# Gated delta rule in a hybrid mixer block: products of two heads that alternate between row tiles, a recurrence on full 128x128 tiles, and the masked q.k products written as one run

## The chip, the cores and the metric

The kernel runs on one core of a Trainium2 chip. A core has a matrix engine (TensorE, PE in the profile; its weight loads are listed apart as PEld), VectorE (DVE), ScalarE (ACT), GpSimd (POOL) and SyncE (SP), each with a queue of its own that it works off in order. The metric is the device time of one execution in microseconds.

## The reference, cut to what matters

One layer for 512 tokens of width 1024: a norm, a wide projection, four token mixers side by side (a gated delta rule, latent attention, gated linear attention, forgetting attention), gates and a merge, an output projection, and a two-layer MLP. The change touches the gated delta rule, with 4 heads of 64 channels and 8 chunks of 64 tokens:

```python
def gated_delta_rule(q, k, v, g, beta):           # chunks of C = 64 tokens
    gc = cumsum(g over the chunk)
    diff = gc[..., :, None] - gc[..., None, :]
    decay_ts = where(lower, exp(diff), 0)
    kk = einsum('bhncd,bhnsd->bhncs', kc, kc)
    a_strict = where(strict, beta * kk * decay_ts, 0.0)
    # (u | w) = (I + a_strict)^-1 (v * beta | k * beta * exp(gc))
    qk = einsum('bhncd,bhnsd->bhncs', qc, kc) * decay_ts
    q_decay = qc * exp(gc);  k_tail = kc * exp(gc[-1] - gc);  chunk_decay = exp(gc[-1])

    def step(state, inp):                          # one chunk after the other
        v_new = u_c - einsum('bhck,bhkv->bhcv', w_c, state)
        o_c = einsum('bhck,bhkv->bhcv', qd_c, state) + einsum('bhcs,bhsv->bhcv', qk_c, v_new)
        state = state * cd_c + einsum('bhck,bhcv->bhkv', kt_c, v_new)
        return state, o_c
```

## The kernel before

Everything is float32. Large projections are split into high and low parts and computed as three products of 512 columns (mm3, L246, weights whi and wlo; the cast that makes whi is L149 on ScalarE, the subtraction that makes wlo is L150 on VectorE). Small products are plain float32; each of them is two passes on TensorE, which the profile counts as two matmuls. A product may use the whole 128x128 array, or a part of it: a row tile of 64 rows (64\*128 in the rows) when the contraction has 64 elements, or a column tile (128\*64) when the output has 64 partitions. Which part is chosen follows from the partitions at which the operands and the output lie. Heads are kept in pairs: pair p holds head 2p on partitions 0 to 63 and head 2p+1 on 64 to 127.

The order on each engine is set by a scheduler that interleaves the products of the gated delta rule with projections of the other branches (L246, accumulators acc): it sorts the code by its own priorities, and the projections fill TensorE while VectorE and ScalarE work for the small steps. Outputs of small products go around a ring of six PSUM banks, b0 to b5 (ps_sm).

The stages of the gated delta rule, in order:

- the gates: softplus, a scan into RF (L424, L427), the rows RS, and their transposes (L441) into cols.
- decay_mat, once per head for A and once for QK: a selector product over 512 columns (L458) spreads the head's row, VectorE adds columns and mask, ScalarE takes the exponential, and four products per head (L469, row tile of 64, one bank per head) give the part that VectorE multiplies with it.
- decayed q, and token-layout k and v by transposes (L507, multiplied by VectorE at L509).
- the inverses of 32x32 blocks (VectorE and DMAs), and 64x64 inverses by products L616 from tiles XD (made at L601).
- u (L638, full array) and wT (L646, column tile of 64) per head, four products each.
- the recurrence, chunk by chunk: wT times state (L665), the subtraction in place in u (L669), q times state (L673), k-tail times u (L678, row tile of 64), the update of the state on VectorE in four steps of 64x64 (L683). The state Sb is kept block diagonal for a pair of heads. After every second chunk come the masked q.k products (L689), which add to the bank of L673, and two copies on ScalarE (L692).
- the gate of the linear attention (L710, then a chain of VectorE and ScalarE to the transposes L737) and the forgetting attention (scores L757, probabilities transposed at L770) follow in code and are interleaved with the above.

Of the kernel before, what the change touches and what calls it, by code (L numbers as in the profile page):

```python
# [35 lines left out]
# columns of w_in  # L36
# [5 lines left out]
# columns of the constants  # L42
# [10 lines left out]
# columns of the per-channel vectors  # L53
# [4 lines left out]
def constants():  # L58
# [19 lines left out]
    # rows of the row tile: 0-3 q norm, 4-7 k norm, 36-39 chunk tail, 96-99 fox, 100-103 gate, 104-107 beta  # L78
# [27 lines left out]
    # rows of the stacked row tile: 0-31 norms hi, 32-63 norms lo, 64-95 gates lo, 96-127 gates hi  # L106
# [14 lines left out]
def hybrid_mixer_kernel(ctx, tc, I, out):  # L121
# [8 lines left out]

    def ps_acc():
        return psp.tile([P, 512], F32, name="acc", tag="acc", bufs=2)
# [19 lines left out]
    # the tensor engine's clock rises with use  # L152
# [64 lines left out]
    def raw_cols(w, c0):  # L217
        """[128, 8, 128] of the columns of a [1024, n] matrix"""
# [75 lines left out]
    def rows_4k(c0, a):  # L294
        """[128, 4, 256] of w_in"""
# [25 lines left out]
    def fslot(i, name, dt=F32):  # L321
        """the places of the keys and queries of FOX, then of GLA's tiles, then of the branches' high parts"""
# [19 lines left out]
    def selector(kind, i):  # L342
        """one-hot rows against all 128 outputs (kind 0, 1: head i) or each half's head (2, 3: pair i)"""
# [9 lines left out]
    # token layout: gla_v | fox_v  # L353
# [11 lines left out]
    def silu(dst, src):  # L365
        """dst = src * sigmoid(src)"""
# [6 lines left out]
    def softplus(dst, z, rows):  # L373
        """dst = max(z, 0) + log1p(exp(-|z|)) on the given partitions"""
# [4 lines left out]
        # series for small arguments  # L379
# [26 lines left out]
    # rows: 0-31 kpe, 32-63 kpe with its halves swapped, 64-79 gla_lr, 96-99 fox_f, 100-103 dn_a, 104-107 dn_b  # L406
# [48 lines left out]
    # A^T and (q k)^T per head, [key, (tile, query)]  # L455
    def decay_mat(kind, h, mask, rhs_i, dst):
        ps = ps_sm()
        pe.matmul(out=ps, lhsT=selector(kind, h), rhs=RS, start=True, stop=True)  # L458
        w_ = tmp("dec")
        for j in range(NT):  # L460
            js = slice(j * P, (j + 1) * P)
            dve.scalar_tensor_tensor(out=w_[:, js], in0=ps[:, js], scalar=cols[:, j, h:h + 1], in1=cv(mask),
                                     op0=ALU.add, op1=ALU.add)
        act.activation(out=w_, in_=w_, func=AF.Exp)
# [16 lines left out]
    for h in range(H):  # L481
        decay_mat(0, h, "maskA", 2, AT[h])
# [4 lines left out]
    for h in range(H):  # L487
        QK.append(slot("QK", "QK", 4))
        decay_mat(1, h, "maskQ", 0, QK[h])

    # decayed q, transposed, in the place of q
# [8 lines left out]
    # token layout: k times beta and decay, v times beta (in the places of k and v), k times tail decay  # L500
# [14 lines left out]
    def gate_proj(bi, zc0):  # L515
        """silu of the projected output gate"""
# [34 lines left out]
    def gslot(n):  # L551
        """the place of the n-th gate"""
# [16 lines left out]
    # inverses of the diagonal 32x32 blocks of I + A^T, half of a block's columns to a partition  # L569
# [36 lines left out]
    # (I + A)^-1 transposed, from the inverses of its 32-blocks  # L606
# [4 lines left out]
    def times_at(h, src):  # L611
        """the chunks' products, one above the other"""
# [16 lines left out]
    for h in range(H):  # L629
# [20 lines left out]
    # recurrence over chunks; the state is kept block diagonal for each pair of heads  # L650
# [3 lines left out]
    for i in range(2):  # L654
        s_ = br.tile([P, 2, P], F32, name=f"Sb{i}")
        pool.memset(s_, 0.0)
        Sb.append(s_)
    for n in range(NCH):
        j, o = n // 2, n % 2
        rs = slice(C * o, C * o + C)  # L660
        cur, nxt = Sb[n % 2], Sb[(n + 1) % 2]
        if n > 0:
            psv = ps_sm()
            for p in range(2):
                pe.matmul(out=psv[rs, p * P:(p + 1) * P], lhsT=wT[p][:, C * n:C * n + C], rhs=cur[:, p], start=p == 0,  # L665
                          stop=p == 1, skip_group_check=True)
            for p in range(2):
                uj = u[p][rs, j * P:(j + 1) * P]
                dve.tensor_tensor(out=uj, in0=uj, in1=psv[rs, p * P:(p + 1) * P], op=ALU.subtract)  # L669
        if o == 0:  # L670
            pso = ps_sm()
        for p in range(2):
            pe.matmul(out=pso[:, p * P + C * o:p * P + C * o + C], lhsT=cur[:, p], rhs=qd[p][:, C * n:C * n + C],  # L673
                      start=o == 0 and p == 0, stop=False, skip_group_check=True)
# [10 lines left out]
        if o == 1:  # L685
            js = slice(j * P, (j + 1) * P)
            for h in range(H):
                p, e = h // 2, h % 2
                pe.matmul(out=pso[C * e:C * e + C, p * P:(p + 1) * P], lhsT=u[p][:, j * P + C * e:j * P + C * e + C],  # L689
                          rhs=QK[h][:, js], start=False, stop=h == 3, skip_group_check=True)  # L690
            for p in range(2):
                act.copy(out=oT[p][:, js], in_=pso[:, p * P:(p + 1) * P])  # L692

    def head_norm(bi, gain_row, oT):
        """rms norm over each head's channels, times the gate"""
# [9 lines left out]
    # gated linear attention: gates, decayed queries and keys  # L705
# [75 lines left out]
    # forgetting attention: 64 channels, then the rows (f_q, 1) against (1, -f_k)  # L781
# [347 lines left out]
```

## Time and profile before

| what | value |
|---|---|
| median of three timed runs | 912.97 us (908.45 to 916.18) |
| profiled execution, span | 906.0 us |
| TensorE busy | 891.2 us, 98% |
| VectorE busy | 443.2 us, 49% |
| ScalarE busy | 393.4 us, 43% |
| GpSimd busy | 113.5 us, 13% |

The profiled execution is one of its own; its time is the span from its first instruction to its last. The busy time of an engine is the sum of its instructions without overlap, so an engine with a share near one is either the bound or stands in instructions that take longer than their work. The chain that ended last follows back from the last instruction to what released each one.

### The profile page before, as it was taken

Reading aid. Unit: us, or ns where it says so; the run is one execution under the profiler, and the core shown is the slowest. Engines: PE = TensorE matmul, PEld = TensorE weight load, DVE = VectorE, ACT = ScalarE, POOL = GpSimd, SP = SyncE. Lnnn points to the kernel's source line nnn. Section 1 sums busy time; section 2 is a strip of 40 time slices with the busy share of each in tenths; the row PEclk is TensorE's granted clock in tenths of the full one; section 3 lists DMA queues with packets and bytes.
Section 4 is the critical chain, followed back from the end, with each engine's and each line's share of the span. In section 5 each row is a group of like instructions: output and inputs, shape, how many; then the busy total and the mean of one; then the engine's idle time right before and its main releaser. Section 6 shows DMA issues by size and latency. Waiting matters only on the chain.

```text
span 906.0 us, 11146 instructions
## 1 busy us (share of the span) xinstructions
PE 891.2 (98%) x4407; PEld 724.1 (80%) x4407; DVE 443.2 (49%) x717; ACT 393.4 (43%) x685; POOL 113.5 (13%) x96
## 2 busy tenths in 40 slices
PE   7999999999999999999999999999999999999997
PEld 6987788877667777888888789888888888888885
DVE  6378797436866775443336467322222233333324
ACT  6346453423886764445543355333222333222222
POOL 3100020100000002221124200422332200000000
PEclk9999999999999999999999999999999999999999
DMA  7333244501121012333333732333333333323202
GB/s 261 105 94 93 58 93 110 118 24 39 55 60 47 26 53 67 112 93 94 93 95 92 237 87 70 115 96 94 93 95 102 130 116 94 93 93 94 93 1 93
DMA packets 123699, 83.30 MB, mean 92 GB/s; under 512 B 19488, under 2 KB 115760, under 8 KB 123648
## 3 DMA queue, kind: packets, MB, share of 16 engines
q1 hardware_dynamic: 117696, 77.03, 29.5%
q10 hardware_dynamic: 5696, 4.73, 1.7%
q0 software_dynamic: 256, 0.85, 0.3%
q8 instruction: 34, 0.56, 0.2%
q14 instruction: 17, 0.14, 0.1%
HBM read 79.69 MB, written 2.88 MB: 91 GB/s over the span
## 4 chain that ended last, share of the span: by engine, by line
PE 94%; DVE 2%; ACT 1%; DMA 1%; POOL 1%; issue 0%; ACTq 0%; DVEq 0%; POOLq 0%
PE acc L246 57%; PE b L246 24%; PE b L757 2%; PE b L777 2%; PE b L278 1%; PE b L469 1%; PE b L770 1%; DMA raw<-in_w_out_dram 1%; PE b L616 1%; PE b L673 1%; PE b L801 1%; PE b L678 1%; POOL gate L959 1%; PE b L665 1%; PE b L646 0%
## 5 line engine op out<-in xcount | busy, mean ns | idle before, releaser
L150 DVE TENSOR_TENSOR wlo<-raw,whi 128x1024 fp32r<-128x1024 f32 x134 | 172.8, 1293 | 264.2 <-ACT whi L149 263.9
L149 ACT CAST whi<-raw 128x1024 fp32r<-128x1024 f32 x136 | 142.4, 1050 | 272.4 <-PE acc L246 238.7
L246 PE MATMUL acc<-hl,whi 128*128 128x512 f32 x416 | 165.4, 398 | 0.0
L246 PE MATMUL acc<-hh,whi 128*128 128x512 f32 x416 | 165.2, 397 | 0.0
L246 PE MATMUL acc<-hh,wlo 128*128 128x512 f32 x416 | 164.1, 394 | 0.0
L246 PE MATMUL acc<-h2l,whi 128*128 128x512 f32 (+1 forms) x240 | 91.8, 383 | 0.0
L246 PE MATMUL acc<-h2h,whi 128*128 128x512 f32 (+1 forms) x240 | 91.8, 382 | 0.0
L246 PE MATMUL acc<-h2h,wlo 128*128 128x512 f32 (+1 forms) x240 | 91.7, 382 | 0.0
L246 PEld LDWEIGHTS acc<-hl,whi 128*128 128x128 f32 x416 | 78.4, 188 | 16.6 <-issue 1.2
L246 PEld LDWEIGHTS acc<-hh,whi 128*128 128x128 f32 x416 | 78.2, 188 | 16.2 <-issue 1.1
L246 PEld LDWEIGHTS acc<-hh,wlo 128*128 128x128 f32 x416 | 78.2, 188 | 15.6 <-issue 0.4
L246 PE MATMUL b<-wlo,whi 128*128 128x512 f32 x192 | 74.8, 389 | 0.0
L246 PE MATMUL b<-whi 128*128 128x512 f32 x192 | 74.8, 389 | 0.0
L246 PE MATMUL b<-whi,wlo 128*128 128x512 f32 x192 | 74.7, 390 | 0.0
L246 PEld LDWEIGHTS acc<-h2h,whi 128*128 128x128 f32 x240 | 45.1, 188 | 8.8
L246 PEld LDWEIGHTS acc<-h2h,wlo 128*128 128x128 f32 x240 | 45.1, 188 | 8.7
L246 PEld LDWEIGHTS acc<-h2l,whi 128*128 128x128 f32 x240 | 45.1, 188 | 8.6
L959 POOL TENSOR_TENSOR gate<-gate 128x512 f32<-128x512 f32 x16 | 22.6, 1416 | 189.2 <-DVE gate L957 189.2
L246 PEld LDWEIGHTS b<-whi,wlo 128*128 128x128 f32 x192 | 36.1, 188 | 7.8 <-DVE wlo L150 0.4
L246 PEld LDWEIGHTS b<-wlo,whi 128*128 128x128 f32 x192 | 36.1, 188 | 7.5
L246 PEld LDWEIGHTS b<-whi 128*128 128x128 f32 x192 | 36.1, 188 | 7.4
L1035 POOL TENSOR_TENSOR u<-u 128x512 f32<-128x512 f32 x16 | 25.7, 1604 | 110.3 <-ACT u L1034 110.1
(312 smaller groups left out, 1413.8 us busy)
## 6 DMA issues: line engine op xcount, KB each, us to landing
raw<-in_w_gate_dram SPq DMA_DIRECT2D x32, 512.0 KB, 3.8
raw<-in_w_mlp_in_dram SPq DMA_DIRECT2D x32, 512.0 KB, 4.2
raw<-in_w_mlp_out_dram SPq DMA_DIRECT2D x32, 512.0 KB, 3.5
raw<-in_w_in_dram SPq DMA_DIRECT2D x23, 512.0 KB, 3.9
raw<-in_w_branch_up_dram SPq DMA_DIRECT2D x8, 512.0 KB, 3.9
raw<-in_w_out_dram SPq DMA_DIRECT2D x8, 512.0 KB, 3.5
x_t<-in_x_dram SPq DMA_DIRECT2D x4, 512.0 KB, 7.5
x<-in_x_dram ACTq DMA_DIRECT2D x1, 2048.0 KB, 12.3
```

The costliest lines, as they stand in the source:

```text
L149: act.copy(out=hi, in_=src)
L150: eng.tensor_tensor(out=lo, in0=src, in1=hi.bitcast(F32), op=ALU.subtract)
L246: pe.matmul(out=ps, lhsT=a, rhs=b, start=first and i == 0, stop=last and i == 2, skip_group_check=True)
L278: pe.transpose(out=ps[:, k * P:(k + 1) * P], in_=(src if late else sq)[:, ks], identity=ident)
L469: pe.matmul(out=ps2[:, js], lhsT=qkvT[2 + p][r, js], rhs=qkvT[rhs_i + p][r, js], start=j == 0, stop=j == NT - 1, skip_group_check=True)
L616: pe.matmul(out=pv[:, j], lhsT=av[h][:, j], rhs=src[:, j], start=j == 0, stop=j == NT - 1, skip_group_check=True)
L665: pe.matmul(out=psv[rs, p * P:(p + 1) * P], lhsT=wT[p][:, C * n:C * n + C], rhs=cur[:, p], start=p == 0, stop=p == 1, skip_group_check=True)
L673: pe.matmul(out=pso[:, p * P + C * o:p * P + C * o + C], lhsT=cur[:, p], rhs=qd[p][:, C * n:C * n + C], start=o == 0 and p == 0, stop=Fals ...
L757: pe.matmul(out=ps[:, 0:n], lhsT=qT[e][0:rows, j * P:n], rhs=kT[e][0:rows, 0:n], start=True, stop=True)
L777: pe.matmul(out=psb[C * e:C * e + C, 0:P], lhsT=vt(k, 2 * p + e), rhs=pts[e][:, k * P:(k + 1) * P], start=k == 0, stop=k == j)
L959: pool.tensor_tensor(out=g, in0=g, in1=gts[4 * m + i - 1], op=ALU.add)
L1035: pool.tensor_tensor(out=dst, in0=dst, in1=dst, op=ALU.mult)
```

## The change

Decay products: decay_pair takes a pair of heads. Both selector products and their VectorE and ScalarE steps come first, then eight products, two per token tile, that alternate between the head on partitions 64 to 127 and the one on 0 to 63, into two banks; in_order ties them to that order on TensorE without a semaphore. The passes of L469 are L481 after the change, the selectors L458 are L467, the projections L246 are L252.

wT: the weights of the product are all 128 columns of kbg (L659), of whose output the head's half is copied.

Recurrence: wT times state uses all 128 columns (L688). The subtraction writes its half to vn (L691), a tile of 128x2x128 for odd and one for even chunks whose other half stays zero (in the places of XD); GpSimd copies the half back to u (L693), in the first chunk ScalarE copies u to vn (L696). k-tail times vn is then a product over all 128 partitions (L700). The state update is L705. q times state (L709) adds to two fixed banks, b2 and b3, each for four chunks; the ring has the other four banks meanwhile. The masked q.k products (L718) are written behind the loop, in one order, and four copies of 128x256 (L723) take the place of eight of 128x128. The gate of the linear attention is L743, its transposes L770.

The diff also strips comments. Its core:

```diff
+    def in_order(made):
+        for a, b in zip(made, made[1:]):
+            tc.add_manual_dep(b.ins, a.ins.name, mybir.DependencyInfo(mybir.DependencyClass.NoSync,
+                                                                      mybir.DependencyReason.DATA), reason="in_order")
...
-    def decay_mat(kind, h, mask, rhs_i, dst):
-        ps = ps_sm()
-        pe.matmul(out=ps, lhsT=selector(kind, h), rhs=RS, start=True, stop=True)
-        w_ = tmp("dec")
...
-        p, r = h // 2, slice(C * (h % 2), C * (h % 2) + C)
-        ps2 = ps_sm()
-        for j in range(NT):
-            js = slice(j * P, (j + 1) * P)
-            pe.matmul(out=ps2[:, js], lhsT=qkvT[2 + p][r, js], rhs=qkvT[rhs_i + p][r, js], start=j == 0,
-                      stop=j == NT - 1, skip_group_check=True)
-        dve.tensor_tensor(out=dst, in0=ps2, in1=w_, op=ALU.mult)
+    def decay_pair(kind, p, mask, rhs_i, dsts):
+        ws_ = []
+        for h in (2 * p, 2 * p + 1):
...
+            act.activation(out=w_, in_=w_, func=AF.Exp)
+            ws_.append(w_)
+        ps2 = [ps_sm(), ps_sm()]
+        made = []
         for j in range(NT):
             js = slice(j * P, (j + 1) * P)
+            for e in (1, 0):
+                r = slice(C * e, C * e + C)
+                made.append(pe.matmul(out=ps2[e][:, js], lhsT=qkvT[2 + p][r, js], rhs=qkvT[rhs_i + p][r, js],
+                                      start=j == 0, stop=j == NT - 1, skip_group_check=True))
+        in_order(made)
+        for e in range(2):
+            dve.tensor_tensor(out=dsts[e], in0=ps2[e], in1=ws_[e], op=ALU.mult)
...
-            hs = slice(j * P + C * e, j * P + C * e + C)
-            pe.matmul(out=ps[C * e:C * e + C, js], lhsT=kbg[p][:, hs], rhs=y[:, js], start=j == 0, stop=j == NT - 1,
+            pe.matmul(out=ps[:, js], lhsT=kbg[p][:, js], rhs=y[:, js], start=j == 0, stop=j == NT - 1,
...
+    vn = []
+    for o in range(2):
+        v_ = br.tile([P, 2, P], F32, name=f"vn{o}", tag=f"XD{o}")
+        pool.memset(v_[half[1 - o]], 0.0)
+        vn.append(v_)
+    banks["ring"] = ("b0", "b1", "b4", "b5")
+    psO = [ps_sm("b2"), ps_sm("b3")]
...
-                pe.matmul(out=psv[rs, p * P:(p + 1) * P], lhsT=wT[p][:, C * n:C * n + C], rhs=cur[:, p], start=p == 0,
+                pe.matmul(out=psv[:, p * P:(p + 1) * P], lhsT=wT[p][:, js], rhs=cur[:, p], start=p == 0,
...
-                dve.tensor_tensor(out=uj, in0=uj, in1=psv[rs, p * P:(p + 1) * P], op=ALU.subtract)
+                dve.tensor_tensor(out=vn[o][rs, p], in0=u[p][rs, js], in1=psv[rs, p * P:(p + 1) * P], op=ALU.subtract)
+            for p in range(2):
+                pool.tensor_copy(out=u[p][rs, js], in_=vn[o][rs, p])
+        else:
+            for p in range(2):
+                act.copy(out=vn[o][rs, p], in_=u[p][rs, js])
...
-                pe.matmul(out=psk[:, p * P:(p + 1) * P], lhsT=ktl[p][rs, j * P:(j + 1) * P], rhs=u[p][rs, j * P:(j + 1) * P],
+                pe.matmul(out=psk[:, p * P:(p + 1) * P], lhsT=ktl[p][:, js], rhs=vn[o][:, p],
...
+        for p in range(2):
+            q0 = 256 * (j % 2) + p * P + C * o
+            pe.matmul(out=psO[j // 2][:, q0:q0 + C], lhsT=cur[:, p], rhs=qd[p][:, C * n:C * n + C],
+                      start=n % 4 == 0 and p == 0, stop=False, skip_group_check=True)
+
+    made = []
+    for i in range(2):
+        for j in (2 * i, 2 * i + 1):
             for h in range(H):
...
+                made.append(pe.matmul(out=psO[i][C * e:C * e + C, q0:q0 + P], lhsT=u[p][:, j * P + C * e:j * P + C * e + C],
+                                      rhs=QK[h][:, j * P:(j + 1) * P], start=False, stop=j % 2 == 1 and h == 3,
+                                      skip_group_check=True))
+        pv = psO[i].rearrange("q (j p c) -> q j p c", j=2, p=2)
+        for p in range(2):
+            act.copy(out=oT[p][:, 256 * i:256 * i + 256].rearrange("q (j c) -> q j c", j=2), in_=pv[:, :, p])
+    in_order(made)
+    banks["ring"] = ("b0", "b1", "b2", "b3", "b4", "b5")
```

How the order on TensorE moves shows in two places. The first is the decay stage. Before, two heads' products (b_ names a bank's buffer, qkvT holds k and q, RS and selt are the rows and the selector, hh and hl the two parts of the normed input):

```order
L246 MATMUL acc<-hl,whi 128x512
L469 MATMUL b_889<-qkvT 128x128 x4
L458 MATMUL b_900<-RS,selt 128x512
L246 MATMUL acc<-hh,wlo 128x512
L246 MATMUL acc<-hh,whi 128x512
L246 MATMUL acc<-hl,whi 128x512
L246 MATMUL acc<-hh,wlo 128x512
L469 MATMUL b_910<-qkvT 128x128 x4
L458 MATMUL b_917<-RS,selt 128x512
```

After, at the same stage (two heads in one run):

```order
L252 MATMUL acc<-hh,wlo 128x512
L252 MATMUL acc<-hh,whi 128x512
L481 MATMUL b_884<-qkvT 128x128
L481 MATMUL b_883<-qkvT 128x128
L481 MATMUL b_884<-qkvT 128x128
L481 MATMUL b_883<-qkvT 128x128
L481 MATMUL b_884<-qkvT 128x128
L481 MATMUL b_883<-qkvT 128x128
L481 MATMUL b_884<-qkvT 128x128
L481 MATMUL b_883<-qkvT 128x128
L467 MATMUL b_901<-RS,selt 128x512
```

Two groups of four products, each between projections, have become one run of eight that alternates between two banks, with the selectors of the next pair behind it.

The second place is the recurrence. Before, chunk 3 with its masked products (Sb is the state; L678 is the product with k-tail):

```order
L665 MATMUL b_1689<-Sb_1677,wT 64x128
L673 MATMUL b_1679<-qkvT,Sb_1677 128x64
L665 MATMUL b_1689<-Sb_1677,wT 64x128
L673 MATMUL b_1679<-qkvT,Sb_1677 128x64
L246 MATMUL acc<-hh,wlo 128x512
L246 MATMUL acc<-hh,whi 128x512
L678 MATMUL b_1696<-qkvT,ktl 128x128 x2
L689 MATMUL b_1679<-QK,qkvT 64x128 x4
L246 MATMUL acc<-hl,whi 128x512
```

After, the same chunk, in which the scheduler has put the first eight of the masked products:

```order
L252 MATMUL acc<-hh,wlo 128x512
L688 MATMUL b_1728<-Sb_1677,wT 128x128 x2
L709 MATMUL b_1683<-qkvT,Sb_1677 128x64 x2
L718 MATMUL b_1683<-QK,qkvT 64x128
L700 MATMUL b_1735<-vn_1681,ktl 128x128
L718 MATMUL b_1683<-QK,qkvT 64x128 x2
L700 MATMUL b_1735<-vn_1681,ktl 128x128
L718 MATMUL b_1683<-QK,qkvT 64x128 x5
L252 MATMUL acc<-hh,whi 128x512
```

L665 and L673 alternated; their successors L688 and L709 stand two and two. The masked products, four at the end of the chunk before, are eight in this chunk now, with the two L700 among them; the other eight L718 stand at the last chunk.

## Rows read from the trace of the kernel before

**Rows 1.** The page: the span, TensorE's share and instructions, and the chain that ended last by engine.

```profile
span 906.0 us, 11146 instructions
PE 891.2 (98%) x4407; PEld 724.1 (80%) x4407; DVE 443.2 (49%) x717; ACT 393.4 (43%) x685; POOL 113.5 (13%) x96
...
PE 94%; DVE 2%; ACT 1%; DMA 1%; POOL 1%; issue 0%; ACTq 0%; DVEq 0%; POOLq 0%
```

**Rows 2.** TensorE's waits: line, releaser: total us, times, longest.

```profile
PE b L441 <- DVE RF L427: 0.7, 1, 0.7
...
PE b L770 <- DVE prob L767: 0.3, 1, 0.3
```

**Rows 3.** Timeline of TensorE around a decay group: start, us, line, tile shape, count.

```profile
83.98 0.39 PE L246 MATMUL acc<-hh,whi 128*128 128x512 f32 x1
84.30 1.16 PE L469 MATMUL b<-qkvT 64*128 64x128 f32 x8
...
85.73 0.39 PE L246 MATMUL acc<-hh,wlo 128*128 128x512 f32 x1
```

**Rows 4.** Chain that ended last: start, us, what.

```profile
90.47 1.24 DVE wlo L150
...
95.63 0.04 issue
95.67 1.06 PE b L441 x8
...
169.66 3.52 PE b L616 x32
```

**Rows 5.** Groups by line, 95.6 to 115.1 us, TensorE: count, busy us, mean ns, idle before.

```profile
L469 PE MATMUL b<-qkvT 64*128 64x128 f32 x48 | 7.5, 289 | 0.0
```

**Rows 6.** Timeline of TensorE, u and wT of the first heads.

```profile
177.97 1.06 PE L638 MATMUL b<-qkvT,ATs 128*128 128x64 f32 x8
178.96 1.09 PE L646 MATMUL b<-ATs,qkvT 128*64 128x128 f32 x8
179.98 1.11 PE L638 MATMUL b<-qkvT,ATs 128*128 128x64 f32 x8
```

**Rows 7.** Stretches: busy us of PE, PEld, DVE, ACT, POOL; clock; DMA share; GB/s.

```profile
95.60:115.10 19.50, 19.43 (x101) 14.46 (x102) 14.66 (x43) 10.71 (x27) 2.59 (x3) 1.00 0.23 45
...
186.10:216.70 30.60, 30.60 (x169) 20.02 (x168) 13.25 (x47) 6.94 (x14) 0.00 (x0) 1.00 0.06 18
```

**Rows 8.** Groups by line, the recurrence (186.1 to 216.7 us), TensorE.

```profile
L246 PE MATMUL acc<-hh,wlo 128*128 128x512 f32 x15 | 6.5, 430 | 0.0
...
L673 PE MATMUL b<-qkvT,Sb 128*128 128x64 f32 x32 | 6.1, 293 | 0.0
L678 PE MATMUL b<-qkvT,ktl 64*128 64x128 f32 x28 | 5.5, 305 | 0.0
L665 PE MATMUL b<-Sb,wT 128*64 128x128 f32 x28 | 5.4, 293 | 0.0
L689 PE MATMUL b<-QK,qkvT 128*64 128x128 f32 x32 | 2.6, 285 | 0.0
```

**Rows 9.** Timeline of VectorE in chunk 3; in brackets idle time before and releaser.

```profile
195.64 0.99 DVE L683 SCALAR_TENSOR_TENSOR Sb<-Sb,cd,b 64x64 f32<-64x64 f32 x4 [1.67 <-PE b L678]
198.07 0.50 DVE L669 TENSOR_TENSOR qkvT<-qkvT,b 64x128 f32<-64x128 f32 x2 [1.44 <-PE b L665]
198.78 1.23 DVE L150 TENSOR_TENSOR wlo<-raw,whi 128x1024 fp32r<-128x1024 f32 x1 [0.21 <-issue]
```

**Rows 10.** Groups by line, whole program, GpSimd.

```profile
L959 POOL TENSOR_TENSOR gate<-gate 128x512 f32<-128x512 f32 x16 | 22.6, 1416 | 189.2 <-DVE gate L957 189.2
...
L797 POOL MEMSET gat<- 128x512 f32 x4 | 2.1, 527 | 106.2 <-PE b L757 106.2
```

**Rows 11.** Timeline of TensorE, the gate of the linear attention.

```profile
209.17 1.12 PE L710 MATMUL b<-pelr,gup 32*128 32x512 f32 x2
...
226.52 0.60 PE L737 MATMUL b<-cst,gz 128*128 128x128 f32 x4
```

More of the change, by code (lines that the diff above doesn't have):

```diff
@@ L453, in hybrid_mixer_kernel @@
     act.activation(out=cd.rearrange("p a n -> p (a n)"), in_=ps[:, 0:2 * NCH], func=AF.Exp)
-    def decay_mat(kind, h, mask, rhs_i, dst):
-        ps = ps_sm()
-        pe.matmul(out=ps, lhsT=selector(kind, h), rhs=RS, start=True, stop=True)
-        w_ = tmp("dec")
+    def decay_pair(kind, p, mask, rhs_i, dsts):
+        ws_ = []
+        for h in (2 * p, 2 * p + 1):
+            ps = ps_sm()
+            pe.matmul(out=ps, lhsT=selector(kind, h), rhs=RS, start=True, stop=True)
+            w_ = tmp("dec")
+            for j in range(NT):
+                js = slice(j * P, (j + 1) * P)
+                dve.scalar_tensor_tensor(out=w_[:, js], in0=ps[:, js], scalar=cols[:, j, h:h + 1], in1=cv(mask),
+                                         op0=ALU.add, op1=ALU.add)
+            act.activation(out=w_, in_=w_, func=AF.Exp)
+            ws_.append(w_)
+        ps2 = [ps_sm(), ps_sm()]
+        made = []
         for j in range(NT):
             js = slice(j * P, (j + 1) * P)
-            dve.scalar_tensor_tensor(out=w_[:, js], in0=ps[:, js], scalar=cols[:, j, h:h + 1], in1=cv(mask),
-                                     op0=ALU.add, op1=ALU.add)
-        act.activation(out=w_, in_=w_, func=AF.Exp)
-        p, r = h // 2, slice(C * (h % 2), C * (h % 2) + C)
-        ps2 = ps_sm()
-        for j in range(NT):
-            js = slice(j * P, (j + 1) * P)
-            pe.matmul(out=ps2[:, js], lhsT=qkvT[2 + p][r, js], rhs=qkvT[rhs_i + p][r, js], start=j == 0,
-                      stop=j == NT - 1, skip_group_check=True)
-        dve.tensor_tensor(out=dst, in0=ps2, in1=w_, op=ALU.mult)
+            for e in (1, 0):
[5 more added lines that the diff above has]
+            dve.tensor_tensor(out=dsts[e], in0=ps2[e], in1=ws_[e], op=ALU.mult)
     dram = ctx.enter_context(tc.tile_pool(name="dram", bufs=1, space=bass.MemoryType.DRAM))
@@ L480, in hybrid_mixer_kernel @@
     AT = [flat(ATs, h) for h in range(H)]
-    for h in range(H):
-        decay_mat(0, h, "maskA", 2, AT[h])
+    for p in range(2):
+        decay_pair(0, p, "maskA", 2, AT[2 * p:2 * p + 2])
     for b in range(4):
@@ L485, in hybrid_mixer_kernel @@
         sp.dma_start(out=d_a[:, b].rearrange("g s c -> s g c"), in_=ATs[bs, :, bs])
-    for h in range(H):
-        QK.append(slot("QK", "QK", 4))
-        decay_mat(1, h, "maskQ", 0, QK[h])
+    for p in range(2):
+        QK += [slot("QK", "QK", 4) for _ in range(2)]
+        decay_pair(1, p, "maskQ", 0, QK[2 * p:2 * p + 2])
     qd = qkvT[0:2]
@@ L657, in hybrid_mixer_kernel @@
         Sb.append(s_)
+    vn = []
[5 more added lines that the diff above has]
+    psO = [ps_sm("b2"), ps_sm("b3")]
     for n in range(NCH):
         j, o = n // 2, n % 2
-        rs = slice(C * o, C * o + C)
+        rs = half[o]
+        js = slice(j * P, (j + 1) * P)
         cur, nxt = Sb[n % 2], Sb[(n + 1) % 2]
@@ L684, in hybrid_mixer_kernel @@
                                              in1=psk[es, p * P + C * e:p * P + C * e + C], op0=ALU.mult, op1=ALU.add)
-        if o == 1:
-            js = slice(j * P, (j + 1) * P)
+        for p in range(2):
+            q0 = 256 * (j % 2) + p * P + C * o
[4 more added lines that the diff above has]
+        for j in (2 * i, 2 * i + 1):
             for h in range(H):
                 p, e = h // 2, h % 2
[L689 to L692, printed above, removed]
+                q0 = 256 * (j % 2) + p * P
+                made.append(pe.matmul(out=psO[i][C * e:C * e + C, q0:q0 + P], lhsT=u[p][:, j * P + C * e:j * P + C * e + C],
+                                      rhs=QK[h][:, j * P:(j + 1) * P], start=False, stop=j % 2 == 1 and h == 3,
+                                      skip_group_check=True))
+        pv = psO[i].rearrange("q (j p c) -> q j p c", j=2, p=2)
+        for p in range(2):
+            act.copy(out=oT[p][:, 256 * i:256 * i + 256].rearrange("q (j c) -> q j c", j=2), in_=pv[:, :, p])
+    in_order(made)
+    banks["ring"] = ("b0", "b1", "b2", "b3", "b4", "b5")
     def head_norm(bi, gain_row, oT):
```

6 lines of the change are left out of this document (removed).

## The prediction

> **What bounds the kernel now.** I read the page's shares first. TensorE is busy 891.2 of the 906.0 us span, and the chain that ended last is 94% TensorE, 2% VectorE [rows 1]. So the question of every edit is how much time it takes from TensorE's own queue, and whether TensorE then finds its next operand ready. The second view is what TensorE waited for: in the stages that the diff touches there is one wait that counts, 0.7 us at L441 for the scan of the gates (RF, L427) [rows 2]. In the recurrence there is none: TensorE is busy 30.60 of 30.60 us, VectorE 13.25, GpSimd 0.00, at granted clock 1.00 [rows 7]. A full TensorE queue may still hold lost time, and the timeline shows it.
>
> **What a change of array shape costs.** Projection products (L246, full array, 512 columns) start 0.227 us apart. A group of eight passes of L469 on a row tile of 64 stands between two of them: L246 at 83.98, L469 at 84.30, an L246 behind it, and the one after that at 85.73 [rows 3]. From 83.98 to 85.73 are 1.75 us; two L246 take 0.45 and eight passes 8 x 0.111 = 0.89 (0.111: 32 passes of L616 in 3.52 us, [rows 4]), so 0.40 us are left for going to the row tile and back, 0.20 a change. At L638/L646 full passes and column-tile passes alternate in eights: L638 at 177.97, L646 at 178.96, the next L638 at 179.98 [rows 6]. Sixteen passes take 2.01 us where 16 x 0.111 = 1.77 is work: 0.12 a change, and up to 0.14 in the pairs behind. The recurrence mixes both kinds. In its 30.56 us stand 45 L246 (10.2; three rows of 15, of which one is shown), 88 passes of L665, L673 and L678 (9.8), 32 passes of L689 that run in pairs (1.8) and one L710 (0.9, two passes of 512 columns at four times 0.111) [rows 8], together 22.7; some 7.9 us are left for the 45 changes of shape that I count in the order of before: 0.17 each, between the two direct readings. Over the program I count 146 changes before and 87 after.
>
> **The change part by part.**
>
> *Decay products, second to fourth groups of a pair (L469 to L481).* The first pair (0.4 to 1.3 us) saves nothing: behind it TensorE runs into the wait at 95.67, and VectorE's chain up to there (wlo at 90.47 at the latest, then the steps to RF) is its own queue back to back [rows 4]. After 95.67 eight trips to the row tile become three: 5 x 0.40 = 2.0 us. Then the pairing: 48 passes [rows 5] alternate between row tiles 64 and 0, in two banks. No two different row tiles ever follow each other in the trace of before, so this price is bounded. Column tiles that follow each other do overlap: 32 passes of L689 are busy 2.6 us where 32 of L673 are busy 6.1 [rows 8], the second of a pair a few ns behind the first. At that rate 48 x 0.111 / 2 = 2.7 us are saved. The other end is below nothing: if entering a tile cost its 0.20 us each time, the 48 would lose up to 9 us more; against it, nothing drains between the two column tiles of L689, whose shape changes as much. I take 2.7, the row nearest in kind, and keep 0 in the range. VectorE works 14.66 of the 19.50 us of this stage [rows 7], so it has 4.8 us of room, about what TensorE would gain; I take off 0.3 for single steps that come late. **4.4 us.**
>
> The Trainium skill, "TensorE: Matmul & The Clock Gate", Part 3 (What overlaps and what doesn't), says that a weight load overlaps products in flight only when its row group differs; by it the alternation would get its 2.7 us and the L689 pairs, which share their row group, would not have overlapped. The trace shows that they did, so the rule does not settle the price here.
>
> *L646 to L659.* The weights are the full 128x128 tile; the passes stay 8 per head at 128 columns. The alternation has no change of shape any more: 8 x 0.14 = **1.1 us** (0.12: 1.0). ACT copies the same half. In this stretch TensorE is the only busy engine.
>
> *Recurrence.* L665, L673 and L678 become L688, L709 and L700 with the same number of passes and columns: nothing in work. Changes of shape go from 45 to 12: 33 x 0.17 = 5.6 us. Of the 12, six lie in one place, where the scheduler puts the first eight masked products (L718) around the two L700 of one chunk. What comes in: (a) The subtraction L691 writes vn in place of u, same size as L669. (b) GpSimd copies vn back to u, 14 copies of 64x128; no such copy is in the trace. Bounds: a memset of 128x512 takes 527 ns, a two-operand step of 128x512 takes 1416 ns [rows 10]. I take about 0.5 us. Only L718 reads u, so nobody waits for it, except the first L718 run: it needs two copies right after L691 of its chunk, some 0.5 us of wait. (c) Eight ACT copies become four of double width, off the path. (d) Clearing the halves of vn that stay zero goes to GpSimd in the places of XD, before the loop; it is idle there. (e) One chunk now: L688, L709, two L700, five to seven L246, some 3.0 us of TensorE; VectorE's circle per chunk is L669 0.50 and L683 0.99 [rows 9], and TensorE's L688 and L700 (0.44 each) between them with four hand-overs of 0.04 [rows 4], some 2.5 to 3.0 us. So the circle just fits; the two wlo of 1.23 us that lie in VectorE's queue here [rows 9] can each hold a chunk up. For all waits 1.0 us. 5.6 - 1.0 = **4.6 us.**
>
> The Trainium skill speaks against this part: "TensorEngine Tiling (Array Packing)", Performance Considerations (When to Use Tiling), wants products of contraction 64 as two row tiles side by side, up to twice as fast, and the change takes L678, which has contraction 64, to the full array. The row shows a row-tile pass of L678 at the price of a full one, since both products of a chunk stand in the same row tile; nothing is given up. Were they paired, an estimate by the page would be 28 x 0.111 / 2 = 1.6 us.
>
> *Behind the recurrence.* Six fewer changes among the branches that follow: 6 x 0.17 = 1.0 us. Against it: the gate of the linear attention (L710, now L743) starts early relative to the projections, and its transposes (L737, now L770) follow after 17.35 us [rows 11]. By the order of the change 53 projection products and L743 lie between, 53 x 0.227 + 0.9 + 0.2 = 13.1 us, and none of the recurrence. If the chain of VectorE and ACT between them needs as long as before, TensorE waits 4 us; without the recurrence's VectorE steps in its way (two pairs of L669 and one L683, some 1.9 us by [rows 9]) and its waits for TensorE (of the kind of the 1.44 and 1.67 us there) it needs less. Bounds 0 and 4.0; I take 1.0. **Net 0.**
>
> **Sum.** 4.4 + 1.1 + 4.6 + 0 = 10.1 us of the profiled 906.0, which then is 895.9. The profiled execution's time is its span; the three timed runs lie 2.4 to 10.2 us above it. I take the saving off their median: 912.97 - 10.1 = **902.9 us.** It is 1.1%, and about 1% (9 us) is what a measurement of this kernel can tell from no change.
>
> **Rivals.**
> 1. *Alternating row tiles do not overlap.* 2.7 us less: 905.6. For it: no row of before shows row overlap. Against: column tiles do.
> 2. *The recurrence becomes bound by VectorE.* For it: circle and filler are both near 3.0 us, the two-bank shrinking of the ring (six to four) and two wlo steps. A chunk at 3.7 us instead of 3.0 costs 7 x 0.7 = 4.9: 907.8. Against it: VectorE is busy 13.25 of 30.60 us.
> 3. *Slower than before: the branch that follows becomes the bound.* The first score of the forgetting attention (L757, right behind the recurrence) now comes behind 70 more products, some 4.2 us later against the projections' progress; if the softmax chains of both attentions then end later than the projections that cover them, the gain up to there (10 us) is lost and 4.2 come on top: 917. It decides once the projections run out before the last score of a branch. Against: TensorE waited 0.3 us in all there, once, at L770 [rows 2].
> 4. *The change does not do what it says.* The run of masked products is not at the end: half of it stands in chunk 3. It is in the sum; if TensorE stands there for two slow copies of 1.4 us it costs 2.3 us more: 905.2.
>
> **How the numbers follow.** Forecast 0.50, spread over 899 to 905 since every term has some 20%; rival 1 0.18; rival 2 0.15; rival 3 0.07; rival 4 0.05; the rest, 0.05, is a larger gain (more overlap, no wait): 898. Below 903.8 (faster by over 1%) lie six tenths of the forecast, a part of the rivals 1 and 4, and the rest: 0.45. Within 1%: 0.48. Slower by over 1%: 0.07, rival 3. The median that the sum starts from is one of runs 908.45 to 916.18 apart, which may shift all by some 3 us; so 897 to 910.5 holds 8 in 10.
>
> **What would show it.** Right: 48 passes of L481 at about 0.06 us each, the second of a pair a few ns after the first; L659 and its neighbour at 0.111 us a pass; no L246 gap beside L688 and L700; a recurrence of about 26 us; no more than 1 us of waits in it. Wrong: L481 at 0.111 us or more; waits for vn or Sb in every chunk; waits of TensorE between 210 and 345 us.

## The result, and the profile after

The changed kernel takes 900.6 us (median of four runs, 898.88 to 900.83) against 913.4 us (four runs, 908.45 to 916.18) of the kernel before; the ratio is 0.9868, with a 95% interval of 0.9831 to 0.9904. The forecast was 902.9 us in a range of 897 to 910.5, faster by 10.1 us.

The medians say 12.8 us, the two profiled executions 8.9 us (906.0 and 897.1). Both are true: of 50 executions of the kernel before, 29 had a span of 904.9 to 907.5 us at a mean granted clock of 0.998 or 0.999, and 21 one of 910.7 to 913.0 at 0.992 or 0.993; the profiles of before are all of the first kind, the medians mix both. The 29 average 906.3 us, the four executions of the changed kernel 898.3, which is 8.0 us less. What follows explains the 8.9 between the profiles.

The page of the changed kernel: the span, the engines' busy time, and the chain that ended last by engine (before: [rows 1]).

```profile
span 897.1 us, 11163 instructions
PE 879.0 (98%) x4407; PEld 720.4 (80%) x4407; DVE 441.4 (49%) x717; ACT 394.0 (44%) x683; POOL 118.5 (13%) x112
...
PE 92%; DVE 3%; ACT 1%; DMA 1%; POOL 1%; issue 1%; ACTq 0%; DVEq 0%; POOLq 0%
```

TensorE has as many instructions as before and is busy 12.2 us less; VectorE's and ScalarE's busy times hardly move. The bound is the same engine, and what was saved was not work: the same number of instructions stand closer together, or side by side.

Where it was saved is seen by counting the projection products (L246, now L252; 3,498 in both traces) and comparing the starts of the n-th one (n counts from 0):

```
n       before    after    difference
48       23.88    22.86      -1.02
408      96.59    95.61      -0.97     behind the gates' transposes
480     125.98   122.17      -3.81     behind the decay stage
672     172.99   169.18      -3.81     ahead of u and wT
1056    359.04   350.09      -8.95     behind the attention of the other branches
3480    895.19   886.28      -8.91     end
```

The first 1.02 us are not the change: they stand there after 24 us, ahead of everything that was edited, and product 48 starts 1.7 us apart in the five profiles of the kernel before and 3.1 us apart in the nine of the changed kernel and its variants, some earlier and some later than before. The first decay pair gives nothing, the rest of the decay stage 2.84 us, all that lies between product 672 and 1056 another 5.14. Together, with the 0.04 us lost behind product 1056, 7.9 us are the change's own in these two traces.

TensorE's waits between 85 and 350 us in the changed kernel (before: [rows 2]):

```profile
PE b L252 <- ACT prob L798: 1.7, 1, 1.7
PE b L447 <- DVE RF L433: 1.7, 1, 1.7
PE b L252 <- ACT brh L155: 1.0, 1, 1.0
PE b L770 <- DVE gz L763: 0.4, 1, 0.4
```

The wait for RF has grown from 0.7 to 1.7 us, and three waits that were not there or were 0.3 us stand behind the recurrence.

A decay group in TensorE's timeline (before: [rows 3]): sixteen passes of two heads that alternate.

```profile
105.43 0.39 PE L252 MATMUL acc<-hh,wlo 128*128 128x512 f32 x1
105.75 1.16 PE L481 MATMUL b<-qkvT 64*128 64x128 f32 x16
106.84 0.50 PE L467 MATMUL b<-RS,selt 128*128 128x512 f32 x1
```

From 105.75 to 106.84 are 1.09 us, as long as eight passes took before (84.30 to 85.39): two row tiles do run side by side, and the way into the group and out of it still costs 0.2 us each, once for sixteen passes.

But behind the longer wait the clock falls. Stretches of the changed kernel (columns as in [rows 7], the number behind POOL is the granted clock):

```profile
96.20:99.30 3.10, 3.10 (x10) 2.45 (x9) 1.69 (x4) 1.60 (x7) 0.00 (x0) 0.50 0.26 59
99.30:102.00 2.70, 2.70 (x13) 2.11 (x11) 2.40 (x9) 1.65 (x5) 0.00 (x0) 0.98 0.42 127
```

At 0.50 (1.2 GHz) a product of 512 columns starts 0.427 us after the one before instead of 0.227; 3.1 us at half the clock are some 1.6 us lost. The kernel before has no such stretch in its profile.

u and wT in the timeline (before: [rows 6]):

```profile
174.16 1.06 PE L652 MATMUL b<-qkvT,ATs 128*128 128x64 f32 x8
175.06 1.11 PE L659 MATMUL b<-ATs,qkvT 128*128 128x128 f32 x8
176.00 1.00 PE L652 MATMUL b<-qkvT,ATs 128*128 128x64 f32 x8
```

Sixteen passes take 1.84 us where they took 2.01; the four heads together 7.20 us (174.16 to 181.36) instead of 8.17.

A chunk of the recurrence, TensorE (the columns of tile shape all read 128\*128 now):

```profile
186.15 0.66 PE L688 MATMUL b<-Sb,wT 128*128 128x128 f32 x4
186.65 0.56 PE L709 MATMUL b<-qkvT,Sb 128*128 128x64 f32 x4
187.01 0.48 PE L252 MATMUL acc<-hh,wlo 128*128 128x512 f32 x1
187.33 0.38 PE L700 MATMUL b<-vn,ktl 128*128 128x128 f32 x2
187.47 0.48 PE L252 MATMUL acc<-hh,whi 128*128 128x512 f32 x1
187.79 0.38 PE L700 MATMUL b<-vn,ktl 128*128 128x128 f32 x2
...
189.17 0.65 PE L688 MATMUL b<-Sb,wT 128*128 128x128 f32 x4
```

And VectorE and GpSimd in the same chunk and the next (before: [rows 9]):

```profile
186.85 0.48 DVE L691 TENSOR_TENSOR vn<-qkvT,b 64x128 f32<-64x128 f32 x2 [0.66 <-PE b L688]
188.21 0.99 DVE L705 SCALAR_TENSOR_TENSOR Sb<-Sb,cd,b 64x64 f32<-64x64 f32 x4 [0.88 <-PE b L700]
...
190.46 1.23 DVE L156 TENSOR_TENSOR wlo<-raw,whi 128x1024 fp32r<-128x1024 f32 x1
```

```profile
187.19 0.56 POOL L693 COPY qkvT<-vn 64x128 f32<-64x128 f32 x2 [2.48 <-DVE vn L691]
190.28 1.56 POOL L693 COPY qkvT<-vn 64x128 f32<-64x128 f32 x2 [2.54 <-DVE vn L691]
```

A chunk takes 3.02 us; VectorE waits twice in it for TensorE, 0.66 and 0.88 us, and TensorE for nobody. From 181.36 to 206.37 the recurrence takes 25.01 us with 49 projection products in it; before, 30.56 with 45 and L710. Without L710 and its two changes of shape (an estimate of 1.3: two passes of 0.44 and two changes of some 0.2) and with 45 products in both that is 29.3 against 24.1: 5.2 us.

### The profile page after: what moved, and what is told of

Its sections match the earlier page's. It is cut to its first block, busy times and chain, and to the rows that moved or that the text cites. A ratio compares the mean times of both kernels' runs of the same rounds, so it can differ in the third digit from the quotient of the medians.

```text
span 897.1 us, 11163 instructions
## 1 busy us (share of the span) xinstructions
PE 879.0 (98%) x4407; PEld 720.4 (80%) x4407; DVE 441.4 (49%) x717; ACT 394.0 (44%) x683; POOL 118.5 (13%) x112
## 4 chain that ended last, share of the span: by engine, by line
PE 92%; DVE 3%; ACT 1%; DMA 1%; POOL 1%; issue 1%; ACTq 0%; DVEq 0%; POOLq 0%
PE acc L252 56%; PE b L252 24%; PE b L790 2%; PE b L810 2%; PE b L284 1%; PE b L803 1%; DMA raw<-in_w_out_dram 1%; DVE wlo L156 1%; PE b L630 1%; PE b L834 1%; POOL gate L992 1%; PE b L481 0%; ACT whi L155 0%; PE b L659 0%; PE b L700 0%
## 5 line engine op out<-in xcount | busy, mean ns | idle before, releaser
L252 PE MATMUL acc<-hh,whi 128*128 128x512 f32 x416 | 165.6, 398 | 0.1
L252 PE MATMUL acc<-hh,wlo 128*128 128x512 f32 x416 | 165.1, 397 | 0.0
L252 PE MATMUL acc<-hl,whi 128*128 128x512 f32 x416 | 164.1, 394 | 0.0
L252 PEld LDWEIGHTS acc<-hh,wlo 128*128 128x128 f32 x416 | 78.4, 189 | 17.1 <-issue 1.8
L252 PE MATMUL acc<-h2l,whi 128*128 128x512 f32 (+1 forms) x240 | 91.8, 382 | 0.0
L252 PE MATMUL acc<-h2h,whi 128*128 128x512 f32 (+1 forms) x240 | 91.7, 382 | 0.0
L252 PE MATMUL acc<-h2h,wlo 128*128 128x512 f32 (+1 forms) x240 | 91.7, 382 | 0.0
L252 PEld LDWEIGHTS acc<-hh,whi 128*128 128x128 f32 x416 | 78.5, 189 | 16.0 <-ACT gate L577 0.4
L252 PEld LDWEIGHTS acc<-hl,whi 128*128 128x128 f32 x416 | 78.3, 188 | 15.3 <-issue 0.3
L252 PE MATMUL b<-wlo,whi 128*128 128x512 f32 x192 | 74.7, 389 | 0.0
L252 PE MATMUL b<-whi 128*128 128x512 f32 x192 | 74.7, 389 | 0.0
L252 PE MATMUL b<-whi,wlo 128*128 128x512 f32 x192 | 74.7, 390 | 0.0
L252 PEld LDWEIGHTS acc<-h2h,wlo 128*128 128x128 f32 x240 | 45.1, 188 | 8.8
L252 PEld LDWEIGHTS acc<-h2l,whi 128*128 128x128 f32 x240 | 45.1, 188 | 8.8
L252 PEld LDWEIGHTS acc<-h2h,whi 128*128 128x128 f32 x240 | 45.1, 188 | 8.6
L252 PEld LDWEIGHTS b<-whi,wlo 128*128 128x128 f32 x192 | 36.0, 188 | 7.8 <-DVE wlo L156 0.4
L252 PEld LDWEIGHTS b<-wlo,whi 128*128 128x128 f32 x192 | 36.0, 188 | 7.6
L252 PEld LDWEIGHTS b<-whi 128*128 128x128 f32 x192 | 36.0, 188 | 7.5
```

What stands on the lines that cost most here:

```text
L252: pe.matmul(out=ps, lhsT=a, rhs=b, start=first and i == 0, stop=last and i == 2, skip_group_check=True)
```

## The experiments

**The kernel before, four more times.** No edit. Once with its runs timed:

> The kernel before once more, unchanged, for its spread. Theory 1 (the profiled 906.0 us of before is its lucky end: its runs spread over 908 to 916): the ratio is 1.00, the runs spread by several us again, and a longer span comes from stretches that the change does not touch, such as the first 20 us. Theory 2 (906.0 is typical): span 905 to 907 and no stretch differs by more than 0.3 us.

The ratio to itself is 0.9981 (0.9949 to 1.0014), span 906.3; the starts of its projection products lie 0.25 to 0.37 us behind the first profile from the 24th to nearly the last. So this profile repeats the first to 0.1 us stage by stage, and its start does not. The ten runs fell into the two kinds named above, six and four. Three more single executions were meant to catch the longer kind:

> The kernel before again, to profile an execution at the level of 912 us. Theory 1: where it happens, the granted clock is 0.50 for some 11 us in one stretch, in the recurrence (186 to 217 us), whose products fill half the array. Theory 2: the low clock is in the decay stage, behind the wait for RF at 95 us, as in the changed kernel, or spread over the whole span.

> The kernel before again, for an execution at its upper level (span 912 us at mean clock 0.993). Theory 1: the lost 6 us lie in three or four stretches of some 3 us at clock 0.50 in the attention behind the recurrence (220 to 345 us), as one of 3 us at 257 us in the kernel with the old recurrence. Theory 2: in the recurrence or the decay stage.

> The kernel before once more, to the same end and with the same two theories: stretches at clock 0.50 in the attention behind the recurrence, or in the recurrence or the decay stage.

Spans 907.5, 906.0 and 907.1, mean clock 0.998 and 0.999: all of the shorter kind, with the wait for RF at 0.7 us in each and no stretch at 0.50 before the very end. Where the other 21 executions lose 6 us remains unseen.

**The first pair head by head.**

```diff
+        order = [(j, e) for j in range(NT) for e in (1, 0)]
+        if (kind, p) == (0, 0):
+            order.sort(key=lambda x: -x[1])
+        for j, e in order:
```

> The changed kernel with one edit: the first pair's eight decay products run head by head instead of alternating, so TensorE has 0.9 us more work ahead of the wait for RF and waits about 0.8 us instead of 1.7. Theory 1 (the long wait is what lowers the clock to 0.50 from 96.0 to 99.3 us in the changed kernel, which costs 1.6 us): granted clock stays 1.00 there, from the start of L447 to the first L630 about 69.3 us instead of 71.0, span about 895.5, although work was added. Theory 2 (the shortfall in the decay stage has to do with the pairs themselves, their banks or VectorE): clock or not, the stretch stays at 71.0 and the span at 897.

The wait fell to 1.1 us and the clock still went to 0.50, from 97.7 to 100.7 us; the products start 0.75 us behind those of the changed kernel at the 48th, 1.31 just ahead of the wait, and 0.76 again behind it and up to the 480th, which is the difference at the start. So 0.6 us of more work on TensorE cost nothing, since it lay in the wait, but the wait was not short enough to part the theories. Median 900.38 us.

**The other three pairs head by head.** The same edit with the condition turned round.

> The changed kernel with one edit: the first pair still alternates, the three others run head by head within the same two banks and with the same number of changes of shape. Theory 1 (products of two row tiles overlap when they alternate): the 48 passes take 0.111 us each again, 2.7 us more; L447 to the first L630 73.7 us, span about 899.8. Theory 2 (the gain of the stage is only the fewer changes of shape): 71.0 and 897.

Behind the decay stage the kernel is 1.41 us later (1.81 us behind the changed kernel at product 408, 3.22 at 480), span 900.2, median 902.22. That is neither 2.7 nor 0. A group in its timeline:

```profile
108.14 1.71 PE L483 MATMUL b<-qkvT 64*128 64x128 f32 x16
109.78 0.73 PE L467 MATMUL b<-RS,selt 128*128 128x512 f32 x2
```

and the distance in ns from each of its passes to the next:

```
213 112 112 111 6 106 108 4 107 4 108 112 111 112 112 201
```

The group takes 1.64 us, not 2.0 (sixteen passes of 0.111 and 0.2 for the way in and out): where the first head's passes end and the second head's begin, three of the one run beside three of the other without being written so. Alternating is worth 0.55 us a group, 1.65 for three; the other 1.0 us of the 2.7 already comes from standing two heads next to each other, which the old order with projections between them did not.

**Both pairs for A ahead of the wait.**

```diff
+    early = [pair_products(p, 2) for p in range(2)]
+    for p in range(2):
+        decay_pair(0, p, "maskA", 2, AT[2 * p:2 * p + 2], early[p])
```

> The changed kernel with the decay products of both pairs for A issued ahead of the selectors, so that sixteen passes more stand ahead of the wait for RF and as many fewer behind it; the wait falls from 1.7 to some 0.2 us. Theory 1 (wait and low clock together cost): no low clock, 1.6 us, and 1.3 us of work moved into the wait: L447 to the first L630 about 68.0 us, span about 894. Theory 2 (no connection of wait and clock): only the 1.3 us, span about 895.8.

Neither came. The scheduler put the gates' transposes behind 398 projection products instead of 408, so TensorE came to the wait 1.2 us early all the same; the clock fell to 0.50 from 97.3 to 100.4 us. Two groups were split by other products and cost further changes of shape; the stage came out 0.9 us longer. Median 900.11. It shows only that the place of the wait is the scheduler's to choose.

**Products of no use in the wait.**

```diff
+    spin = [pe.matmul(out=ps, lhsT=onesr, rhs=hh[:, 0], start=True, stop=True, skip_group_check=True) for i in range(7)]
...
+    in_order([mms[-1]] + spin + [hold])
```

Here mms[-1] is the last projection product ahead of the wait and hold the first of the gates' transposes.

> The changed kernel with seven products of no use (512 columns each, 1.6 us) put ahead of the first L447, in the time in which TensorE waits for RF; their output is overwritten. Theory 1 (the clock falls because TensorE stands still for over 1 us): no wait above 0.3 us there, granted clock 1.00 over 96 to 102 us, L447 to the first L630 about 69.3 us instead of 71.0, span 1.6 us shorter than the changed kernel at the same start, median about 899. Theory 2 (the clock falls for what stands there behind the wait, small products and selectors, or by chance): the clock falls to 0.50 all the same and the median is 900.6 or above.

The wait is gone and the clock is 1.00 throughout the stage. But the kernel gains only 0.3 us on the changed one (1.27 us behind it before the stage, 0.96 after); median 901.27. TensorE now waits for VectorE at other places, and the stretch shows VectorE full:

```profile
PE b L526 <- DVE QK L490: 0.6, 1, 0.6
...
PE b L514 <- DVE QK L490: 0.2, 1, 0.2
```

```profile
96.00:116.00 20.00, 19.21 (x125) 14.76 (x126) 18.97 (x47) 13.89 (x33) 5.47 (x4) 1.00 0.39 60
```

So in the profiled execution the clock followed theory 1, and the time did not: the scheduler had reordered the projections and selectors behind the dummies too. The other three executions have mean clocks of 0.996 and 0.997, no higher than the 0.997 of the changed kernel's profile with its low stretch, so that the clock may have fallen somewhere in them; no trace shows it.

**Copies of vn on VectorE.**

```diff
-                pool.tensor_copy(out=u[p][rs, js], in_=vn[o][rs, p])
+                dve.tensor_copy(out=u[p][rs, js], in_=vn[o][rs, p])
```

> The changed kernel with the copies of vn to u on VectorE, right behind each subtraction. Theory 1 (the circle of a chunk has slack on VectorE, which waits 0.7 and 0.8 us for TensorE in each chunk): chunks stay 3.03 us, except those with a wlo in them (0.3 us each at most), no waits of TensorE. Theory 2 (the circle just fits, as forecast): each chunk is 0.3 to 0.6 us longer, 2 to 4 us in the recurrence.

Theory 1. The two copies take 0.34 to 0.36 us of VectorE in each chunk, its idle time before L705 falls from 0.88 to 0.6 us, and the chunks stay at 3.0 us; over the recurrence the kernel is 0.2 us faster than the changed one. VectorE in one of its chunks:

```profile
188.36 0.48 DVE L691 TENSOR_TENSOR vn<-qkvT,b 64x128 f32<-64x128 f32 x2 [0.66 <-PE b L688]
188.77 0.34 DVE L693 COPY qkvT<-vn 64x128 f32<-64x128 f32 x2
189.72 0.97 DVE L705 SCALAR_TENSOR_TENSOR Sb<-Sb,cd,b 64x64 f32<-64x64 f32 x4 [0.61 <-PE b L700]
```

This execution told something else, too. Up to the recurrence its order on TensorE is that of the changed kernel, and it has the same wait for RF (1.65 us at 97.83), but the clock stayed up:

```profile
97.80:100.80 3.00, 2.98 (x18) 2.67 (x19) 2.24 (x4) 1.67 (x7) 0.00 (x0) 1.00 0.02 2
```

It comes out of the decay stage 1.59 us earlier relative to the changed kernel (3.13 us behind it at product 408, 1.54 at 480). With equal instructions on TensorE that is what the low clock costs there: the stage gives 2.84 us with it and 4.43 without. Three other profiles with the last three pairs alternating and the low clock (the first pair head by head, the masked products at the end, the old recurrence) give 2.84, 2.85 and 2.83.

**The masked products at the end.**

```diff
+            last = pe.matmul(out=psO[j // 2][:, q0:q0 + C], lhsT=cur[:, p], rhs=qd[p][:, C * n:C * n + C],
...
-    made = []
+    made = [last]
```

> The changed kernel with one edit: the first eight masked products are tied behind the last L709, so that all sixteen stand at the end of the recurrence. Theory 1 (each change of shape costs TensorE 0.17 us): four to six changes fewer, 0.7 to 1.0 us off the span. Theory 2 (the masked products in chunk 3 fill time in which TensorE would wait for VectorE): no gain, chunk 3 waits instead, or up to 1 us slower because the end has 0.9 us of products in a row in front of the copies.

From 1.98 us behind the changed kernel at product 672 it comes to 0.62 behind at 1056: 1.36 us saved, 1.34 of it within the recurrence, and no wait there. It is more than theory 1 gave, since the order has eight changes of shape fewer (79 instead of 87), not four to six; at 1.36 / 8 = 0.17 us each the price is the forecast one, here from an edit that changes the order alone. The median, 900.58, doesn't show it, with a start 2 us later in the profile and runs from 898.3 to 901.7.

**The old recurrence with the new decay stage.** The loop of the kernel before in place of the new one, with the ring of six banks; decay_pair and L659 stay.

> The changed kernel with the recurrence and the masked products as they were (row and column tiles, subtraction in u, ring of six banks), and the decay pairs and L659 kept. Theory 1 (by the traces the recurrence and what follows give 4.2 us, and the two levels of the kernel before, spans of 906 and 912 at mean clock 0.998 and 0.993, come from a low clock in the recurrence): span 901.3 at the upper clock, and the runs split into two levels again, some 6 us apart. Theory 2 (the second level comes from the decay stage): one level only, about 903.5 of time in every run.

Ten runs: six with spans of 900.4 to 902.7 (mean clock 0.997 or 0.998) and four of 904.4 to 905.5 (0.994 or 0.995), median 904.39. The profile is one of the latter and shows a low clock at two places, behind the wait for RF and in the attention:

```profile
100.00:104.00 4.00, 4.00 (x13) 3.09 (x12) 2.78 (x10) 2.67 (x9) 0.00 (x0) 0.57 0.49 131
...
258.00:260.00 2.00, 2.00 (x6) 1.12 (x5) 1.77 (x5) 2.00 (x5) 0.00 (x0) 0.50 0.04 8
```

Ahead of the second, from 253 to 257 us, TensorE had no wait but a row of short products (scores, transposes, row tiles of 32). By the decay stage this kernel is 2.7 us better than the kernel before, and 1.1 us more behind L659, as the changed kernel is; the low clock at 258 us takes 1.5 back. The run also prices the new loop: from product 672 to product 740 it and the changed kernel have the same work, but for two passes of the old order's first score (0.24 us), and it takes 5.3 us longer. So some 5.1 us are the recurrence's own. The two kinds of theory 1 came, 3 us apart and not 6, but both theories had the place wrong: the second stretch seen lies in the attention behind the recurrence.

**Three edits together:** masked products last, seven products of no use in the wait, and

```diff
-        dve.tensor_tensor(out=qd[p], in0=qkvT[p], in1=e_, op=ALU.mult)
+        pool.tensor_tensor(out=qd[p], in0=qkvT[p], in1=e_, op=ALU.mult)
```

> The changed kernel with three edits: all masked products at the end of the recurrence, the seven products of no use in the wait for RF, and the two products of q with its decay (128x512 each) on GpSimd instead of VectorE. Theory 1 (behind RF VectorE is the bound of the decay stage, 18.97 us busy of 20 once the clock stays up): VectorE's 1.4 us less make TensorE's waits of 0.8 us there go away; with the 0.3 us of the dummies and the 1.3 us of the masked products the span at equal start falls by some 2.4 us, median about 898. Theory 2 (GpSimd's products slow VectorE down by the port that they share, or TensorE is the bound there): 1.6 us at most, median about 899, or no difference.

Median 898.44 us (six runs, 897.02 to 899.41), ratio to before 0.9865 (0.9831 to 0.9898), 2.2 us under the changed kernel's median. By the products' starts 1.95 us behind the changed kernel before the stage, 0.92 after it, and 0.42 ahead at product 1056: 1.0 in the decay stage, 1.3 in the recurrence, 2.4 in all as theory 1 had it. Of the 1.0, the dummies alone gave 0.3 above; that VectorE's lighter queue gave the other 0.7 is argued from this one run (TensorE's waits for QK fell from 0.8 to 0.2 us). The mean clock is 0.998 or 0.999 in all six runs. It is the fastest of the kernels run here, though two ratios this close to each other don't part it from the changed kernel; the traces do.

## Why the prediction was right, point by point

**The frame held.** TensorE stayed the bound, the work on it stayed equal, and the gain is changes of shape and overlap. The forecast saving of 10.1 us stands between the two traces' 7.9 (without the start) and the medians' 12.8. That the median came out so near is in part luck: the forecast took its saving off a median of 912.97 us, which mixes the two kinds of executions of the kernel before, and against the shorter kind alone the change gives 8 us.

**The first pair: nothing, as forecast.** TensorE came 1 us earlier to the wait for RF and waited 1 us longer. I had missed what this does next: a longer wait can be followed by a lower clock.

**Decay stage: forecast 4.4 us, 2.84 in the profile, 4.43 in the execution with equal instructions whose clock stayed up.** The value taken from the column tiles of L689 was right to a tenth (sixteen passes in the time of eight), so rival 1 is refuted. The 2.0 us for five trips fewer were not varied by themselves; 4.43 without the 2.7 leaves 1.7 for them and the single steps that come late, as forecast. The term failed by something outside it, 1.6 us of low clock. VectorE's room of 4.8 us was real but thin: with another order (the dummies) it was the bound.

The Trainium skill, "TensorE: Matmul & The Clock Gate", Part 3 (Measured speedup vs the span model), puts the start of the next tile some 4 ns behind the one before. The trace agrees, with 4 to 7 ns between passes of the two row tiles. The Trainium skill, "TensorEngine Tiling (Array Packing)", Tiling Modes (Key Properties), says that a change of tiling mode, not of the tile alone, drains the engine. The trace agrees here as well: 0.2 us on entry and on exit of a group, none between its two tiles.

**wT: forecast 1.1, measured 0.97.** The direct reading of [rows 6] gave 1.0.

**Recurrence: forecast 4.6, measured 5.2.** The price per change was right (33 changes, 0.16 us each; 0.17 in the run with the masked products at the end); the 1.0 us taken off for waits was not needed. GpSimd's copies took under 0.3 us each but for one of 1.32, where 0.5 was taken, and nothing waited for them that the trace shows. Rival 2 is refuted: TensorE waits nowhere in the recurrence, VectorE is idle 1.5 us in a chunk of 3.02, and some 0.35 us more of its work in each chunk (the copies of vn) made the recurrence no longer.

**Behind it: forecast 0, a loss of 1.0.** This is what is left of the 5.14 us, not a reading of its own. The six changes of shape saved there were outweighed by waits of 3.1 us (gz 0.4, prob 1.7, brh 1.0) where before there were 0.3; by these figures the loss would be 1.8, and the difference isn't accounted for. I had expected the wait at the gate of the linear attention (0.4 instead of 1.0) and not at the later projections into the small banks (b L252), which wait for ScalarE. Waits of TensorE between 210 and 345 us were named as a sign of being wrong, and this term of the sum was. It looks like rival 3's mechanism at less than a tenth of its size; the old recurrence with the new decay stage has none of these waits but 0.3, and no run took them away alone.

**Rival 4** was true in what it said, eight masked products in chunk 3, and its price is known now: 1.3 us, the eight changes of shape that the order without it lacks. I had counted six of them and half a us of wait, and no wait came.

**What stays open.** It is not known why the same wait of 1.65 us is followed by a low clock in one execution and not in another, nor where the kernel before loses its 6 us in two of five executions: none of these was caught with a trace. The one kernel with the old recurrence and the new decay stage had two kinds of runs 3 us apart, but this doesn't part the two loops: its longer kind has mean clocks of 0.994 and 0.995, and so have five of the 31 executions with the new recurrence, one of the changed kernel itself among them (899.0 us at 0.994).

## What to carry to other kernels

A full TensorE queue hides time between products: count the changes of array shape in the order, price one from two neighbouring starts in the timeline, and choose an order that needs fewer, even if half the array's output is thrown away. Then look at where TensorE will arrive early: a saved us ahead of a wait is a longer wait, and behind it the clock may be at half. Where medians and profiles differ, compare the start of each n-th repeated product in two traces; it parts the stages, the start and the clock, which medians of a few runs mix.

## What was not expected of the hardware

- Behind a wait of TensorE of 1.1 to 1.7 us the clock fell to 0.50 in six of seven profiles, 1 to 3 us after the restart and for some 3 us; behind the wait of 0.7 us in none of five, nor in the two profiles in which dummies filled the wait. The five are all of the shorter kind of the kernel before, so they do not show that its 0.7 us is always harmless.
- Products on two row tiles that stand one after the other in blocks overlap at the seam, three passes deep.
- GpSimd's pair of copies of 64x128 took 1.56 us instead of 0.53 where VectorE ran the subtraction of 128x1024 at the same time (190.28 and 190.46 us). The copy that had started before the subtraction took 0.29 us, the one that started 0.06 us behind it 1.32, and ended 0.15 us after it; so it was in all seven profiles in which the two met in this way.
